# Stores moved from SyncE to ScalarE, gate loads split, and more gathers beside each u block, in a Hymba-style block with a PEER layer

## The chip, the core and the metric

The kernel runs on one core of one Trainium2 chip. The metric is the device time of one execution in microseconds (us), as the median of several runs. In what follows PE is TensorE, DVE is VectorE, ACT is ScalarE, POOL is GpSimd and SP is SyncE, which here only issues DMAs.

## What is computed

One layer on a sequence of 512 tokens with 2048 features: two mixers side by side (forgetting attention and an mLSTM), an output projection, and then a PEER layer, which is where the change lies. PEER picks, for every token, 8 × 16 = 128 of 16384 single-neuron experts, by two top-k searches over product keys:

```
q = (xt @ w_q)                                   # 8 heads, 2 halves of 128
scores = einsum('thpd,pnd->thpn', q, keys)
s_top, i_top = top_k(scores, 16)                 # per half
cand = s_top[0][:, None] + s_top[1][None, :]     # 16 x 16
s_fin, pos = top_k(cand, 16);  gate = softmax(s_fin)
ub = u[idx];  act = gelu(einsum('thkd,td->thk', ub, x)) * gate
vb = v[idx];  y = einsum('thk,thkd->td', act, vb)
out = rmsnorm(x + y)
```

`u` and `v` have 16384 rows of 2048 features.

## The kernel before, in words

The 512 tokens are NT = 4 tiles of 128. Two ways are used for PEER, side by side.

**Sparse way.** For the first tile (128 tokens) and half of the second (NS = 64 tokens) each chosen expert's row is gathered from `u`: 128 gathers for tile 0 and 64 for the half tile, which lies twice on the partitions, so 192 gathers of 128 rows of 8 KB (1 MB). The generator `gathered` (line 626) issues an indirect DMA on POOL (line 633) into one of three `row` buffers and, two steps later (LAG), a dot on DVE (line 643) that multiplies the row with the token's features and sums. Later the same generator gathers `v` rows for tile 0. `advance(n)` (line 685) moves this generator on by n steps. Each gather and each dot is tied by `beside` (line 620) to the last hi cast issued before it, so the steps go at the pace of the dense work.

**Dense way.** The remaining 320 tokens (DU) go through all experts. The experts are NI = 128 blocks of 128. A u block (`early_steps`, lines 592 to 610) streams its 2 × 512 KB of transposed `u` in two halves through `stream_split`: a raw load on SP (line 109, four `raw` buffers), a cast to the high part `hi` on ACT (line 115) and a subtraction that leaves the low part `lo` on DVE (line 117); three buffers each for hi and lo. 48 matmuls of 320 columns (line 122) add hi and lo products into a PSUM tile `sacc`. A Gelu on ACT (line 608) writes the tile `es` (two buffers), and a store puts its 160 KB into the DRAM table `stab` (line 609). Activations are needed only where a token chose an expert; this is what the gates are for.

**Gate tables.** `table` (lines 936 to 961) writes for 32 tokens (TG) a table of all 16384 gates, 2 MB, in eight groups of four tokens: an `on` on DVE (one-hot rows, line 945), four scaled copies `og` on ACT (line 950), eight small matmul records `gp` on PE, a copy into `stg` on ACT (line 953). Three u blocks are interleaved with the eight groups of a table, step by step. The table is then stored to `gtab` (line 957). There are NTG = 12 tables; the first two belong to the half tile that takes its u activations from the sparse way and can be made only when its dots are done.

**The order around the change** is this (times are of the profiled execution). The program asks for:
1. eight w_q heads with seven u blocks each, top-k searches beside them, `advance(PACE_EARLY)` per block (960 to 1506);
2. ten tables, each with three u blocks, each followed by `advance(PACE_G * 3)` (1506 to 1844);
3. u blocks alone, with `advance(PACE_U)` each, until 14 (HOLD) are left (1844 to 2018);
4. whatever is left of the u gathers, at a step per call (line 965; 2018 to 2115). The 14 held-back blocks run beside it, since the scheduler pulls them ahead;
5. the last two tables (lines 973 and 974; 2115 to 2172);
6. the transition: gates and activations come back from DRAM. `load_gates(g)` loads the gates of eight blocks (GB) of all 12 tables into `gtA` or `gtB`; `load_s(k)` loads activations of two blocks, `sv`; `gated(k)` multiplies both into `wv` (line 1000 on ACT for the two sparse tables, line 1002 on DVE for the ten) and splits it into hi and lo parts in `wbufA` or `wbufB` (lines 1006 and 1007) (2172 to 2257);
7. the v products: 16 groups of eight blocks, four `vS` raw loads per pair of blocks, split like u (2257 to 3190).

A tile scheduler fixes each engine's order at build time: it takes what is ready by its own modelled costs and priorities, so an engine's order isn't that of the code. A lo subtraction has a raised priority (AHEAD_LO). On the chip every engine runs its own list strictly in order, and waits at an instruction whose inputs or buffers aren't there. A DMA on SP's list waits in the same way, and everything behind it with it.

Of the kernel before, what the change touches and what calls it, by code (L numbers as in the profile page):

```python
# [36 lines left out]
NS = 64  # L37
# [3 lines left out]
NI = 128  # L41
GB = 8
TG = 32
# [3 lines left out]
EARLY_G = 3  # L47
HOLD = 14
PACE_O = 0.4
PACE_EARLY = 1.15  # L50
PACE_G = 1.5
PACE_U = 1.5
LAG = 2
AHEAD_LO = 35
NTG = ND // TG
# [32 lines left out]
def block_kernel(ctx: ExitStack, tc: tile.TileContext, a, out):  # L88
    nc = tc.nc
# [17 lines left out]
    def stream_split(src, width=1024, to=None):  # L107
        raw = stream.tile([P, 1024], F32, tag="raw", name="raw", bufs=4)
        nc.sync.dma_start(out=raw[:, :width], in_=src)
        if to is None:  # L110
            hi = stream.tile([P, 1024], F32R, tag="hi", name="hi", bufs=3)
            lo = stream.tile([P, 1024], F32R, tag="lo", name="lo", bufs=3)
        else:
            hi, lo = to[:, 0:1024], to[:, 1024:2048]
        pace[0] = nc.scalar.copy(out=hi[:, :width], in_=raw[:, :width]).ins  # L115
        with tc.high_priority(offset=AHEAD_LO):
            nc.vector.tensor_tensor(out=lo[:, :width], in0=raw[:, :width],  # L117
                                    in1=hi[:, :width].bitcast(F32), op=OP.subtract)
        return hi, lo

    def mm(o, l, r, start, stop):
        nc.tensor.matmul(out=o, lhsT=l, rhs=r, start=start, stop=stop)  # L122
# [441 lines left out]
    stab = gdram.tile([NI, P, DU], F32, name="stab")  # L564
    gtab = gdram.tile([NTG, P, NI * TG], F32, name="gtab")
# [4 lines left out]
    def tpool(stack, name, bufs=1, **kw):  # L570
        return stack.enter_context(tc.tile_pool(name=name, bufs=bufs, reuse_waits="tile", **kw))
# [15 lines left out]
    def flat(x):  # L587
        return x.rearrange("p h k -> p (h k)")

    nearly = [0]  # L590

    def early_steps():

        b = nearly[0]
        nearly[0] += 1
        acc = psA.tile([P, 512], F32, tag="acc", name="sacc")[:, 0:DU]
        for s in range(2):
            hi, lo = stream_split(a["uT"][b, s])
            for kk in range(8):
                kc = 8 * s + kk  # L600
                uh, ul = hi[:, kk * P:(kk + 1) * P], lo[:, kk * P:(kk + 1) * P]
                mm(acc, uh, x3d[:, 0, kc, NS:], kc == 0, False)
                mm(acc, uh, x3d[:, 1, kc, NS:], False, False)
                mm(acc, ul, x3d[:, 0, kc, NS:], False, kc == KC - 1)
                if kc % 2 == 1 and kc < KC - 1:
                    yield
        sv = esp.tile([P, DU], F32, tag="es", name="es")
        nc.scalar.activation(out=sv, in_=acc, func=AF.Gelu)
        nc.sync.dma_start(out=stab[b], in_=sv)
        yield  # L610

    def early_s():
        for _ in early_steps():
            pass
# [70 lines left out]
    def advance(n):  # L685
        state[0] += n
        while state[0] >= 1.0:
            state[0] -= 1.0
            done[0] += 1
            next(sparse, None)  # L690

    with ExitStack() as rx:
# [117 lines left out]
        def w_q(h):  # L810

            acc = [psA.tile([P, 512], F32, tag="acc", name="acc") for _ in range(2)]
            for s in range(4):
                hi, lo = stream_split(a["w_q"][h, s])
                for j in range(2):
                    for kk in range(4):
                        kc = 4 * s + kk
                        wh = hi[:, kk * 256 + j * P:kk * 256 + (j + 1) * P]
                        wl = lo[:, kk * 256 + j * P:kk * 256 + (j + 1) * P]
                        mm(acc[j][:, 0:ND], wh, x3d[:, 0, kc, :], kc == 0, False)  # L820
                        mm(acc[j][:, 0:ND], wh, x3d[:, 1, kc, :], False, False)
                        mm(acc[j][:, 0:ND], wl, x3d[:, 0, kc, :], False, kc == KC - 1)
            qT = xq.tile([P, 2, ND], F32, tag="w2", name="qT", bufs=1)
            for j in range(2):
                nc.scalar.copy(out=qT[:, j, :], in_=acc[j][:, 0:ND])
            res = {}
            for t in range(1, NT):
                sc = psB.tile([P, 2, P], F32, tag="ps", name="sc")
                for j in range(2):
                    mm(sc[:, j, :], qT[:, j, (t - 1) * P:t * P], keysT[:, j, :], True, True)  # L830
                res[t] = n2.tile([P, 2, P], F32, tag="scs", name="scs", bufs=4)
                nc.scalar.copy(out=res[t], in_=sc)
            return res
# [63 lines left out]
        for k, _ in enumerate(steps):  # L897
            next(chosen, None)
            if k % 8 == 7:
                advance(PACE_EARLY)  # L900
        for _ in chosen:
            pass
        for h in range(PH):
            scs = w_q(h)
            advance(PACE_EARLY)
            for t in range(1, NT):
                for _ in range(EARLY_TOPK[t - 1]):
                    early_s()
                    advance(PACE_EARLY)
                for _ in choose(t, h, scs[t]):  # L910
# [15 lines left out]
    with ExitStack() as rx:  # L926
        n3 = tpool(rx, "n3", 2)
        idxT = n3.tile([P, 2, ND], F32, name="idxT", bufs=1)
        gT = n3.tile([P, ND], F32, name="gT", bufs=1)
        for dst, src in ((idxT[:, 0], i0f), (idxT[:, 1], i1f), (gT, gts)):  # L930
            pt = psB.tile([P, ND], F32, tag="ps", name="pt")
            for t in range(1, NT):
                nc.tensor.transpose(pt[:, (t - 1) * P:t * P], flat(src[:, t]), ident)
            nc.scalar.copy(out=dst, in_=pt)

        def table(tg, blocks):
            stg = n3.tile([P, NI, TG], F32, tag="stg", name="stg")
            steps = itertools.chain(*[early_steps() for _ in range(blocks)])
            for q4 in range(TG // 4):
                for _ in range(blocks):  # L940
                    next(steps)
                gp_ = psB.tile([P, 4, NI], F32, tag="ps", name="gp_")
                t4 = tg * TG + q4 * 4
                on = n3.tile([P, 2, 4, P], F32, tag="on", name="on")
                nc.vector.tensor_tensor(  # L945
                    out=on, in0=iota[:, None, None, :].to_broadcast([P, 2, 4, P]),
                    in1=idxT[:, :, t4:t4 + 4, None].to_broadcast([P, 2, 4, P]), op=OP.is_equal)
                for q in range(4):
                    og = n3.tile([P, P], F32, tag="og", name="og", bufs=6)
                    nc.scalar.activation(out=og, in_=on[:, 0, q, :], func=AF.Copy,  # L950
                                         scale=gT[:, t4 + q:t4 + q + 1])
                    mm(gp_[:, q, :], on[:, 1, q, :], og, True, True)
                nc.scalar.copy(out=stg[:, :, q4 * 4:q4 * 4 + 4].rearrange("p i q -> p q i"),  # L953
                               in_=gp_)
            for _ in steps:
                pass
            nc.sync.dma_start(out=gtab[tg], in_=stg.rearrange("p i q -> p (i q)"))

        for tg in range(NS // TG, NTG):
            table(tg, EARLY_G)  # L960
            advance(PACE_G * EARLY_G)
        while nearly[0] < NI - HOLD:
            early_s()
            advance(PACE_U if not u_over[0] else 0.0)
        while not u_over[0]:
            advance(1.0)

        pt = psB.tile([P, ND], F32, tag="ps", name="pt")
        nc.tensor.transpose(pt[:, 0:P], act1, ident)
        for r in range(R):  # L970
            rs = slice(r * S1, (r + 1) * S1)
            nc.scalar.copy(out=gT[rs, 0:NS], in_=pt[rs, r * NS:(r + 1) * NS])
        for tg in range(NS // TG):
            table(tg, EARLY_G)
# [3 lines left out]
    wbufs = [va.tile([P, 2, GB, ND], F32R, name="wbufA", bufs=1), None]  # L978
    gtb = [va.tile([P, NTG, GB, TG], F32, name="gtA", bufs=1), None]

    def load_gates(g):
        gt = gtb[g % 2]
        nc.sync.dma_start(out=gt.rearrange("p g i q -> p g (i q)"),
                          in_=gtab[:, :, g * GB * TG:(g + 1) * GB * TG].rearrange("g p x -> p g x"))

    svs = {}

    def load_s(k):

        if k < NI // 2:  # L990
            svs[k] = va.tile([P, 2, DU], F32, tag="sv", name="sv", bufs=3)
            nc.sync.dma_start(out=svs[k], in_=stab[2 * k:2 * k + 2].rearrange("b p x -> p b x"))

    def gated(k):
# [11 lines left out]
        nc.scalar.copy(out=hi, in_=wv)  # L1006
        nc.vector.tensor_tensor(out=lo, in0=wv, in1=hi.bitcast(F32), op=OP.subtract)

    load_gates(0)
    while nearly[0] < NI - 2:  # L1010
        early_s()
    load_s(0)
    load_s(1)
    for k in range(2):
        gated(k)
    while nearly[0] < NI:
# [147 lines left out]
```

## Time and profile before

| what | us |
|---|---|
| median of 3 runs (3238.1 to 3244.2) | 3241.77 |
| the profiled execution | 3246.45 |
| its span | 3244.7 |
| PE busy in it | 3123.0 (96%) |
| DVE busy | 2328.5 (72%) |
| ACT busy | 1281.5 (39%) |
| POOL busy | 604.3 (19%) |

The mean granted clock of PE is 0.984 of its full rate. The stages have different limits, so the shares over the whole span say little; the times of the stages stand in the list above, and the stretches in the rows below are cut along them.

### The profile page before, as it was taken

How to read it: one execution, taken by the hardware profiler on the slowest of the kernel's cores; microseconds unless marked ns; L12 is line 12 of the kernel's file. 1: busy time of each engine (PE TensorE's matmuls, PEld its weight loads, DVE VectorE, ACT ScalarE, POOL GpSimd, SP SyncE). 2: the span in 40 equal slices, each digit the busy share in tenths (PEclk: the TensorE clock that was granted, in tenths of full speed). 3: DMA queues.
4: the chain of work that ended last, by engine and by line, in shares of the span. 5: the costliest groups of instructions: out<-in, count | busy, mean ns of one | idle time of the engine just before them, and what ended most of it. 6: DMA issues, size and time to landing. Idle time of an engine off the chain costs nothing.

```text
span 3244.7 us, 43324 instructions
## 1 busy us (share of the span) xinstructions
PE 3123.0 (96%) x16682; PEld 2752.9 (85%) x16682; DVE 2328.5 (72%) x3251; ACT 1281.5 (39%) x1957; POOL 604.3 (19%) x444
## 2 busy tenths in 40 slices
PE   8999999998989999999899899889999999999998
PEld 6788787787789999999898899877888888888887
DVE  6533333457899999898788787857778877887764
ACT  4432222345443333335777533263333333333332
POOL 0000000100322222222221233302222222222200
PEclk9999999999999999999999999989999999999999
DMA  4232232266868888887888899969988888888853
GB/s 158 72 98 78 78 97 73 78 213 201 317 238 292 298 309 294 305 285 269 320 309 328 331 408 397 387 243 340 335 310 315 324 327 319 311 317 329 300 182 118
DMA packets 220258, 835.71 MB, mean 258 GB/s; under 512 B 21586, under 2 KB 79314, under 8 KB 175954
## 3 DMA queue, kind: packets, MB, share of 16 engines
q1 hardware_dynamic: 173970, 497.38, 44.4%
q0 software_dynamic: 46080, 335.56, 26.9%
q8 instruction: 130, 2.13, 0.3%
q14 instruction: 78, 0.63, 0.1%
HBM read 781.94 MB, written 50.92 MB: 257 GB/s over the span
## 4 chain that ended last, share of the span: by engine, by line
PE 76%; issue 9%; DVE 6%; DMA 4%; POOL 2%; ACT 2%; DVEq 0%; SPq 0%; POOLq 0%; ACTq 0%
PE y L122 23%; PE acc L122 23%; PE sacc L122 17%; PE yk L122 8%; DMA row<-in_u,idx 2%; DVE lo L117 2%; POOL row L633 2%; DVE row L643 1%; PE sps L122 1%; ACT stg L953 1%; ACT og L950 1%; DMA raw<-in_w_out 1%; PE po L122 1%; ACT hi L115 1%; DMA gtA<-gtab 1%
## 5 line engine op out<-in xcount | busy, mean ns | idle before, releaser
L115 ACT CAST hi<-raw 128x1024 fp32r<-128x1024 f32 x736 | 773.6, 1051 | 1537.6 <-PE acc L122 433.3
L117 DVE TENSOR_TENSOR lo<-raw,hi 128x1024 fp32r<-128x1024 f32 x736 | 897.5, 1222 | 589.2 <-ACT hi L115 588.6
L122 PE MATMUL sacc<-x3d,hi 128*128 128x320 f32 x4096 | 934.6, 316 | 0.0
L122 PEld LDWEIGHTS sacc<-x3d,hi 128*128 128x128 f32 x4096 | 697.3, 192 | 0.0
L122 PE MATMUL sacc<-x3d,lo 128*128 128x320 f32 x2048 | 647.4, 316 | 46.1 <-DVE lo L117 45.9
L643 DVE SCALAR_TENSOR_TENSOR row<-row,x 128x2048 f32<-128x2048 f32 x192 | 437.9, 2286 | 64.9 <-DMA row<-in_u,idx 56.7
L122 PEld LDWEIGHTS sacc<-x3d,lo 128*128 128x128 f32 x2048 | 392.0, 191 | 52.1 <-DVE lo L117 52.1
L633 POOL DMA_INDIRECT row<-in_u,idx x192 | 289.9, 1510 | 670.5 <-ACT hi L115 373.5
L633 POOL DMA_INDIRECT row<-in_v,idx x128 | 224.9, 1757 | 767.7 <-ACT hi L115 540.4
L122 PE MATMUL y<-hi,wbufA 128*128 128x512 f32 x1152 | 357.4, 390 | 3.8 <-DVE x L1085 3.8
L122 PE MATMUL y<-hi,wbufB 128*128 128x512 f32 x1128 | 349.0, 389 | 0.0
L672 DVE SCALAR_TENSOR_TENSOR x<-row,dots,x 128x2048 f32<-128x2048 f32 x128 | 300.2, 2345 | 0.0
L122 PEld LDWEIGHTS y<-hi,wbufA 128*128 128x128 f32 x1152 | 217.0, 188 | 49.5 <-DVE x L1085 4.3
L122 PEld LDWEIGHTS y<-hi,wbufB 128*128 128x128 f32 x1128 | 211.7, 188 | 44.0
L122 PE MATMUL acc<-xT,hi 128*128 128x512 f32 x768 | 244.1, 396 | 0.0
L122 PE MATMUL acc<-hi,xT 128*128 128x512 f32 x768 | 241.8, 393 | 0.0
L122 PE MATMUL y<-lo,wbufA 128*128 128x512 f32 x576 | 224.8, 390 | 0.0
L122 PE MATMUL y<-lo,wbufB 128*128 128x512 f32 x564 | 219.4, 389 | 0.0
L162 POOL TENSOR_TENSOR rsr<-rst,mhalf 128x1 f32<-128x1 f32 (+2 forms) x24 | 19.0, 795 | 894.1 <-DVE rst L159 894.1
L122 PEld LDWEIGHTS acc<-xT,hi 128*128 128x128 f32 x768 | 144.2, 189 | 28.5 <-ACT xT L179 0.2
L122 PEld LDWEIGHTS acc<-hi,xT 128*128 128x128 f32 x768 | 143.8, 188 | 28.6
L945 DVE TENSOR_TENSOR on<-cst,idxT 128x1024 f32<-128x1024 f32 x96 | 117.0, 1223 | 47.6 <-PE gp__15151 L122 2.0
(545 smaller groups left out, 4168.6 us busy)
## 6 DMA issues: line engine op xcount, KB each, us to landing
raw<-in_uT SPq DMA_DIRECT2D x256, 512.0 KB
raw<-in_vS SPq DMA_DIRECT2D x256, 512.0 KB
raw<-in_w_out SPq DMA_DIRECT2D x64, 512.0 KB
raw<-in_w_q SPq DMA_DIRECT2D x64, 512.0 KB
gtab<-stg SPq DMA_DIRECT2D x12, 2048.0 KB
stab<-es SPq DMA_DIRECT2D x128, 160.0 KB
sv<-stab SPq DMA_DIRECT2D x64, 320.0 KB
raw<-in_w_fqk SPq DMA_DIRECT2D x32, 512.0 KB
```

Source lines behind the costliest of these rows:

```text
L115: pace[0] = nc.scalar.copy(out=hi[:, :width], in_=raw[:, :width]).ins
L117: nc.vector.tensor_tensor(out=lo[:, :width], in0=raw[:, :width], in1=hi[:, :width].bitcast(F32), op=OP.subtract)
L122: nc.tensor.matmul(out=o, lhsT=l, rhs=r, start=start, stop=stop)
L162: nc.gpsimd.tensor_tensor(out=r, in0=t, in1=mhalf[:, 0:width], op=OP.pow)
L633: beside(nc.gpsimd.indirect_dma_start(out=row, out_offset=None, in_=a[src], in_offset=bass.IndirectOffsetOnAxis(ap=idx(j), axis=0)))
L643: return nc.vector.scalar_tensor_tensor(out=row, in0=row, scalar=1.0, in1=x30, op0=OP.mult, op1=OP.mult, accum_out=to[:, j:j + 1])
L672: return nc.vector.scalar_tensor_tensor(out=x2[:, 0, :], in0=row, scalar=dots[0][:, j:j + 1], in1=x2[:, 0, :], op0=OP.mult, op1=OP.add)
L945: nc.vector.tensor_tensor(out=on, in0=iota[:, None, None, :].to_broadcast([P, 2, 4, P]), in1=idxT[:, :, t4:t4 + 4, None].to_broadcast([P, ...
L950: nc.scalar.activation(out=og, in_=on[:, 0, q, :], func=AF.Copy, scale=gT[:, t4 + q:t4 + q + 1])
L953: nc.scalar.copy(out=stg[:, :, q4 * 4:q4 * 4 + 4].rearrange("p i q -> p q i"), in_=gp_)
```

## The change

The stores of u blocks (line 609) and of gate tables (line 957) are issued by ACT instead of SP: 128 stores of 160 KB and 12 of 2 MB. PACE_EARLY rises from 1.15 to 1.25 gather steps per u block, PACE_G from 1.5 to 1.9. The gates of the first eight blocks are loaded in two parts: the ten tables that are made first, and, after four blocks from the end, the two last ones. The first two `sv` loads stand in the code ahead of the last blocks instead of between them.

```diff
-PACE_EARLY = 1.15
-PACE_G = 1.5
+PACE_EARLY = 1.25
+PACE_G = 1.9
@@ early_steps
         nc.scalar.activation(out=sv, in_=acc, func=AF.Gelu)
-        nc.sync.dma_start(out=stab[b], in_=sv)
+        nc.scalar.dma_start(out=stab[b], in_=sv)
@@ table
-            nc.sync.dma_start(out=gtab[tg], in_=stg.rearrange("p i q -> p (i q)"))
+            nc.scalar.dma_start(out=gtab[tg], in_=stg.rearrange("p i q -> p (i q)"))
@@ load_gates
-    def load_gates(g):
-        gt = gtb[g % 2]
+    def load_gates(g, tgs=slice(0, NTG)):
+        gt = gtb[g % 2][:, tgs]
         nc.sync.dma_start(out=gt.rearrange("p g i q -> p g (i q)"),
-                          in_=gtab[:, :, g * GB * TG:(g + 1) * GB * TG].rearrange("g p x -> p g x"))
+                          in_=gtab[tgs, :, g * GB * TG:(g + 1) * GB * TG].rearrange("g p x -> p g x"))
@@ after the tables
-    load_gates(0)
+    load_gates(0, slice(NS // TG, NTG))
+    while nearly[0] < NI - 4:
+        early_s()
+    load_gates(0, slice(0, NS // TG))
+    load_s(0)
+    load_s(1)
     while nearly[0] < NI - 2:
         early_s()
-    load_s(0)
-    load_s(1)
     for k in range(2):
         gated(k)
```

The paces and the code's order reach the engines through the scheduler. Counted in the two orders: 87 dots stand ahead of the tables before and 94 now; in the ten tables 42 (bursts of four and five in turn) and 53 (bursts of four to six, at most six); beside the dense blocks 38 in both; the leftover stretch has 25 and 7. The last two tables begin on PE at u block 123.6 before (the 16 groups within 2.4 blocks) and at 115.9 now: ten groups within 1.6 blocks, the other six some 18 u matmuls apart, and eight blocks behind the last group.

On DVE, at the end of a table with five dots before; `row` is a gathered row, `dots` the sums, `on` the one-hot rows of a gate group:

```order
L117 TENSOR_TENSOR lo<-raw,hi 128x1024
L643 SCALAR_TENSOR_TENSOR row,dots_4841<-row,x_4830 128x2048
L945 TENSOR_TENSOR on<-cst,idxT 128x1024
L117 TENSOR_TENSOR lo<-raw,hi 128x1024
L643 SCALAR_TENSOR_TENSOR row,dots_4841<-row,x_4830 128x2048
L945 TENSOR_TENSOR on<-cst,idxT 128x1024
L643 SCALAR_TENSOR_TENSOR row,dots_4841<-row,x_4830 128x2048 x3
L117 TENSOR_TENSOR lo<-raw,hi 128x1024
```

On DVE, at the end of a table with six dots now:

```order
L643 SCALAR_TENSOR_TENSOR row,dots_4841<-row,x_4830 128x2048
L945 TENSOR_TENSOR on<-cst,idxT 128x1024
L117 TENSOR_TENSOR lo<-raw,hi 128x1024
L945 TENSOR_TENSOR on<-cst,idxT 128x1024
L643 SCALAR_TENSOR_TENSOR row,dots_4841<-row,x_4830 128x2048 x3
L117 TENSOR_TENSOR lo<-raw,hi 128x1024
L643 SCALAR_TENSOR_TENSOR row,dots_4841<-row,x_4830 128x2048
L945 TENSOR_TENSOR on<-cst,idxT 128x1024
L643 SCALAR_TENSOR_TENSOR row,dots_4841<-row,x_4830 128x2048
L117 TENSOR_TENSOR lo<-raw,hi 128x1024
```

Four dots and an `on` stood between two lo's before; now three and an `on`, then a lo, then two and an `on`.

On SP, where the u blocks end, before; `raw<-in_vS` are the first loads of the v products:

```order
L957 DMA gtab<-stg 128x4096
L109 DMA raw<-in_vS 128x1024
L609 DMA stab<-es 128x320
L983 DMA gtA<-gtab 128x12x256
L992 DMA sv<-stab 128x2x320 x3
L609 DMA stab<-es 128x320
L983 DMA gtB<-gtab 128x12x256
L992 DMA sv<-stab 128x2x320 x3
L109 DMA raw<-in_vS 128x1024
```

On SP at the same place now:

```order
L983 DMA gtA<-gtab 128x12x256
L109 DMA raw<-in_vS 128x1024 x6
L983 DMA gtB<-gtab 128x12x256
L109 DMA raw<-in_vS 128x1024 x2
L992 DMA sv<-stab 128x2x320 x2
L109 DMA raw<-in_vS 128x1024
```

and, some 16 u loads ahead of that, the two parts of the first gates among the u loads:

```order
L109 DMA raw<-in_uT 128x1024 x11
L983 DMA gtA<-gtab 128x10x256
L109 DMA raw<-in_uT 128x1024
L983 DMA gtA<-gtab 128x2x256
L992 DMA sv<-stab 128x2x320 x2
L109 DMA raw<-in_uT 128x1024 x4
L992 DMA sv<-stab 128x2x320 x2
```

The `gtA` of 12 tables ahead of the six `vS` loads is that of the third group of eight blocks; the stores are gone from this list. On DVE all four `gated` pairs of the first eight blocks stand ahead of the last nine lo's of u; before they stood behind all of them.

## Rows read from the trace of the kernel before

**Rows 1.** Windows: us, PE, PEld, DVE, ACT, POOL busy (instructions), PEclk, DMA share, GB/s.
```profile
960.00:1506.00 546.00, 537.78 (x3535) 534.58 (x3536) 495.27 (x1118) 191.48 (x248) 142.69 (x147) 1.00 0.85 297
1619.00:1649.40 30.40, 29.20 (x211) 28.45 (x211) 25.59 (x23) 25.92 (x53) 8.21 (x4) 1.00 0.76 274
1649.40:1683.50 34.10, 31.24 (x210) 30.98 (x210) 27.15 (x24) 23.20 (x47) 6.25 (x5) 0.90 0.96 364
1506.00:1843.90 337.90, 308.28 (x2133) 301.77 (x2132) 262.13 (x230) 248.10 (x498) 73.92 (x44) 0.96 0.83 306
1872.50:2017.80 145.30, 144.48 (x985) 144.22 (x984) 119.76 (x105) 51.13 (x65) 55.14 (x32) 1.00 1.01 402
2017.80:2115.10 97.30, 80.37 (x484) 77.79 (x483) 78.55 (x70) 24.33 (x31) 33.23 (x22) 0.91 0.97 381
2115.10:2172.00 56.90, 53.32 (x362) 48.87 (x360) 30.12 (x27) 46.14 (x99) 1.80 (x1) 1.00 0.56 202
2172.00:2257.10 85.10, 70.83 (x289) 57.44 (x290) 59.83 (x54) 28.25 (x41) 16.11 (x9) 0.90 0.97 349
```
**Rows 2.** Windows of the tile sacc alone: PE, PEld, ACT, PEclk, DMA share, GB/s.
```profile
1506.00:1843.90 337.90, 258.07 (x1493) 229.12 (x1492) 13.77 (x32) 0.96 0.83 306
2017.80:2115.10 97.30, 80.37 (x484) 77.79 (x483) 4.30 (x10) 0.91 0.97 381
2115.10:2172.00 56.90, 44.01 (x233) 35.06 (x231) 2.13 (x5) 1.00 0.56 202
```
**Rows 3.** Chain of work that ended last: start, us, engine, tile, line, instructions.
```profile
1044.47 48.54 PE sacc L122 x331
...
2273.43 48.96 PE y L122 x216
```
**Rows 4.** Timeline of PE, a gate group: start, us, engine, line, operation.
```profile
1517.82 1.05 PE L122 MATMUL gp__13556<-og,on 128*128 128x128 f32 x8
1518.63 0.54 PE L122 MATMUL sacc<-x3d,hi 128*128 128x320 f32 x2
```
**Rows 5.** Timeline of DVE in a table with four dots.
```profile
1630.63 1.22 DVE L117 TENSOR_TENSOR lo<-raw,hi 128x1024 fp32r<-128x1024 f32 x1
...
1639.61 1.22 DVE L117 TENSOR_TENSOR lo<-raw,hi 128x1024 fp32r<-128x1024 f32 x1
```
**Rows 6.** Timeline of DVE in the next table, with five dots; idle before in brackets.
```profile
1659.23 1.22 DVE L117 TENSOR_TENSOR lo<-raw,hi 128x1024 fp32r<-128x1024 f32 x1
...
1667.50 2.29 DVE L643 SCALAR_TENSOR_TENSOR row<-row,x 128x2048 f32<-128x2048 f32 x1 [1.49 <-DMA row<-in_u,idx]
...
1671.00 2.29 DVE L643 SCALAR_TENSOR_TENSOR row<-row,x 128x2048 f32<-128x2048 f32 x1 [1.20 <-DMA row<-in_u,idx]
...
1673.21 1.22 DVE L117 TENSOR_TENSOR lo<-raw,hi 128x1024 fp32r<-128x1024 f32 x1
```
**Rows 7.** Timeline of PE behind that.
```profile
1674.49 0.64 PE L122 MATMUL sacc<-x3d,lo 128*128 128x320 f32 x1 [2.86 <-DVE lo L117]
```
**Rows 8.** Timeline of POOL in the same table: a gather's issue.
```profile
1662.93 1.67 POOL L633 DMA_INDIRECT row<-in_u,idx  x1 [2.81 <-DVE row L643]
```
**Rows 9.** SP: its waits for Gelu (total, times, longest); timeline in that table.
```profile
SPq L609 <- ACT es L608: 170.5, 72, 7.3
...
1649.88 0.33 SPq L609 DMA_DIRECT2D stab<-es  x1
1650.30 6.03 SPq L109 DMA_DIRECT2D raw<-in_uT  x3
...
1669.11 0.33 SPq L957 DMA_DIRECT2D gtab<-stg  x1
```
**Rows 10.** Timelines at the transition, of PE, ACT and SP.
```profile
2181.57 0.80 PE L122 MATMUL yk<-hi,wbufA 128*128 128x512 f32 x1 [10.39 <-ACT wbufA L1006]
...
2177.63 0.50 ACT L1000 COPY wv<-gtA 128x128 f32<-128x128 f32 x2 [5.17 <-DMA gtA<-gtab]
...
2173.99 0.43 SPq L983 DMA_DIRECT2D gtB<-gtab  x1
2185.83 0.46 SPq L109 DMA_DIRECT2D raw<-in_vS  x1
```

## The prediction, made before the changed kernel was run

> **What bounds the kernel now.** I read the page's busy shares first, then the table of time windows by stage, then the chain of waits and the timelines around the waits. TensorE is busy nearly all the time, so the question for each stage is how much longer it lasts than its matmuls need. The units come from long unbroken runs in the chain [rows 3]: 48.54 us for 331 u matmuls is 146.6 ns each, so a u block of 48 takes 7.04 us; 48.96 us for 216 v products is 226.7 ns each. A gate group between u matmuls takes 1518.63 − 1517.82 = 0.81 us [rows 4], a table of eight 6.5 us. By these units [rows 1, 2]:
> - ten tables: 337.9 − 1493 × 0.1466 (218.9) − 10 × 6.5 = 54 us over;
> - dense u blocks: 145.3 for 985 matmuls, 1 us over. Here TensorE is the bound and the gathers beside it (1.5 per block) are free;
> - leftover gathers, 2.5 per block: 97.3 − 484 × 0.1466 (71.0) = 26.3 us over, with the DMA share at 0.97: bound by bytes;
> - last two tables: 56.9 − 233 × 0.1466 (34.2) − 13 = 9.7 us over;
> - transition to the v products: 85.1 − 289 × 0.2267 (65.5) = 19.6 us over.
> The two table rows of 30.4 and 34.1 us [rows 1] are a table with four dots and one with five. One more dot costs 3.7 us there. The timelines say how. In the four-dot table VectorE's longest way between two lo's is 1630.63 to 1639.61, three dots and an `on` [rows 5]; in the five-dot one it is 1659.23 to 1673.21, four dots, of which the last two wait 1.49 and 1.20 us for their rows [rows 6]. TensorE uses up its lo's and pauses 2.86 us [rows 7], and the granted clock of that table is 0.90 instead of 1.00 [rows 1]: if it fell from 2.4 to 1.2 GHz behind the pause, it stayed there for a fifth of 34.1 us and lost half of these 6.8. The pause and 3.4 make 6.3, and the table is over by as much: of its 210 matmuls 64 are of gate groups, and 34.1 − 146 × 0.1466 − 6.5 = 6.2. So the price is that of a pause, not of a dot.
>
> **The change part by part.** Sums are made against the profiled execution, 3246.45 us, which is 4.7 above the median of 3241.77; the forecast starts from the median.
>
> *The stores on ScalarE.* They leave SP's queue, where they waited 170.5 us for Gelu [rows 9] with the raw loads behind them. In the stages that cost nothing visible: three raw loads pass right behind a store [rows 9], and where TensorE stops it waits for lo, not for raw. So the gain in the stages is 0. On ScalarE each store stands right behind the Gelu or the copy that makes its data, so the wait is the engine's own order and only the issue is added, 0.33 us by SP's row [rows 9]. What is queued behind it is the next hi cast, for which lo and then TensorE wait. In the tables about 40 stores make 13 us of work on an engine that is busy 248.1 of 337.9 [rows 1]. From below 0, since it idles 90 us there; from above 13, if each lies in the way. I take a third of the 13, **+4**, as the stops go back to VectorE. Elsewhere ScalarE has over half its time free: 0.
>
> *More gathers beside the w_q heads.* The order has 94 dots ahead of the tables instead of 87: seven more of 2.29 us [rows 6] on a VectorE that is busy 495.27 of 546 [rows 1]. TensorE idles 8.2 us there with 51 us free on VectorE; 16 fewer free add about a quarter, **+2** (0, covered, to 8, doubled).
>
> *More gathers in the ten tables:* 53 dots instead of 42, in bursts of 4 to 6. At 3.7 us each the 11 cost 41, the upper bound. The lower is −8: the order puts a lo after three dots, so the long way of 14 us that made the pauses is gone, and a six-dot table may run like the four-dot one. Between them I take the wait for a row that a late dot shows, 1.20 us [rows 6], VectorE's 2.29 beside it being hidden as in the four-dot table: 11 × 1.2 = **+13**.
>
> *Dense blocks:* 38 dots in both orders, **0**.
>
> *Leftover:* 7 dots instead of 25. The stage loses 26.3/25 = 1.05 us per dot, 18 fewer give **−19** (−24, if so few no longer fill the queues; −14, if the rest run slower). The blocks that run there now run beside the last tables or as dense ones, at 7.04 us: no cost.
>
> *Last two tables:* they begin on TensorE at block 115.9 instead of 123.6; 10 of the 16 groups are still crowded into 1.6 blocks, 6 stand apart among u matmuls. I leave 10/16 of the 9.7: **−4** (−10 to 0).
>
> *First gates in two parts, sv loads earlier.* TensorE's stop of 10.39 us comes from the first wbufA [rows 10], for which ScalarE waited 5.17 us on gtA. In the new order VectorE makes all four pairs of the first eight blocks ahead of the last nine lo's; their weights are ready some four blocks early, and the 10.39 go. The other 9.2 stand beside SP's queue: after a store and gtB at 2173.99, the next vS load comes at 2185.83 [rows 10], though lo's free its buffers sooner. In the new order six vS loads stand ahead of gtB. Most of that goes: **−16** (−8, if the second part waits for its table; −20, all). When it is gone the v products' own TensorE rate is next. The second part waits on SP for the last table's store, with the sv loads and four raw loads queued behind it; the last group is some two blocks (14 us) ahead of it, so I cost that at nothing, and it is a rival.
>
> *Sum:* 2 + 13 + 4 + 0 − 19 − 4 − 16 = **−20**; 3241.8 − 20 = **3222 us**.
>
> **The rivals.**
> (a) *The finer interleave makes the added dots free:* no pause as long as 2.86 us, the clock stays. Tables and stores cost 0: 3222 − 17 = **3205**. For: the granted clock is 1.00 in the four-dot table, whose run of dots is as long as the new one. Against: six rows of 1 MB come within about one block and three row buffers.
> (b) *Every added dot brings its 3.7 us:* 41 in place of 13, 3222 + 28 = **3250**, slower. The place is the end of each table. It decides from 33 us for the 11 dots, 3.0 each, where nothing is left of the gain; from 39.5 it measures as slower. For: the measured step from four to five. Against: it counts one pause, which the new order breaks.
> (c) *The stores, on a queue of their own, stretch the gathers.* A row asked for at 1662.93 [rows 8] is used at 1671.00 [rows 6], 8.07 us later, while raw loads and gathers fill the DMA to 0.96 [rows 1]. A gather that shares with two others and not with one takes half as long again, 12.1: 4.0 us at each of ten tables, 3222 + 40 = **3262**. It decides from (20 + 6.5)/10 = 2.7 us a table. Against: the 2 MB store of a table goes out at 1669.11 [rows 9], when all but the last of the burst's rows are asked for. The Trainium skill, page "DMA: Bandwidth & Descriptors", section "Queues, rings and completion order", states that a DMA engine takes turns between the queue rows that have work, packet by packet, and that ScalarE's row is another than SP's. By that rule the store no longer stands in line with the raw loads but takes a share from the gathers; no row here shows ScalarE's row at work. The same page, section "Issuing engines are not separate DMA queues", expects of such a move only the issue time, and speaks against (c) as much as against any gain from the stores.
> (d) *The end doesn't gain:* SP stands at the second part of the gates until the last store has landed, raw loads and vS loads come late behind it; the transition gives 8, the tables 0: 3222 + 12 = **3234**.
> That the change would not do what it says is no case here: the order shows every move.
>
> **How the numbers follow.** The forecast has 0.44, (a) 0.20, (b) 0.18, (c) 0.08, (d) 0.10. A measurement of this kernel tells about 0.2%, 6.5 us, from no change, so faster is below 3235.3 and slower above 3248.3. Faster: 0.41 of the forecast, 0.20, 0.01 of (b), 0.05 of (d), 0.67. Same: 0.03, 0.08 of (b) and 0.05 of (d), 0.16. Slower: 0.09 of (b) and (c), 0.17. The range runs from 3195, (a) with the tail's terms at their best ends, to 3255, (b) with its spread; it leaves out (c), some of (b) and a little below.
>
> **What would show it.** In the changed kernel's windows: the stretch at 2.5 gathers per block shrinks to some 28 us; the stop ahead of the first v product is under 2 us and no vS load is late behind gtB; tables with six dots take 32 to 36 us. A clock of 0.90 in every table and stops on lo of 3 us speak for (b); the same tables at 30 to 31 us for (a); waits of 3 us and more of dots for their rows, with the store of the table under way, for (c); SP standing at the second gates for (d). Wrong altogether would be a loss in a stage that I cost at nothing: the dense blocks, or the v products, which the change leaves alone.

## The result and the profile after

The changed kernel takes 3285.2 us (3284.3 to 3289.0, 4 runs) against 3240.8 before (3238.1 to 3244.2, 4 runs): a ratio of 1.0139, 95% interval 1.0121 to 1.0156. It is 44 us slower; 20 us faster was forecast. The profiled execution has a span of 3287.2 us.

First, where the time went. The ten tables can be cut in both kernels from their first to their last gate group. These are windows of the kernel before, then of the one after; the columns are those of [rows 1].

```profile
1512.30:1832.70 320.40, 293.95 (x2047) 287.97 (x2047) 254.86 (x223) 241.44 (x487) 73.06 (x43) 0.96 0.83 306
```
```profile
960.00:1506.00 546.00, 540.77 (x3538) 536.71 (x3537) 508.36 (x1128) 190.99 (x248) 175.00 (x153) 0.99 0.86 310
1512.70:1902.70 390.00, 314.77 (x2023) 301.92 (x2023) 274.80 (x241) 238.60 (x487) 88.59 (x52) 0.89 0.76 278
1928.00:2103.00 175.00, 170.35 (x1152) 168.58 (x1151) 140.17 (x124) 58.09 (x72) 63.34 (x38) 1.00 1.00 390
2103.00:2125.00 22.00, 17.56 (x101) 17.02 (x99) 17.54 (x17) 6.16 (x12) 3.42 (x3) 0.84 0.90 320
2125.00:2172.00 47.00, 44.30 (x316) 42.19 (x316) 26.52 (x22) 42.59 (x90) 0.00 (x0) 1.00 0.49 176
2172.00:2229.00 57.00, 57.00 (x391) 56.98 (x390) 25.96 (x24) 23.99 (x34) 1.80 (x1) 1.00 0.86 299
2229.00:2314.00 85.00, 81.72 (x357) 66.43 (x356) 64.43 (x56) 29.28 (x39) 18.52 (x11) 1.00 0.94 344
```

The tables take 390.0 us instead of 320.4, with a granted clock of 0.89 instead of 0.96. Of the 70 us, 49 are time in which TensorE stands still (75 us now, 26 before), and 21 are longer busy time at the lower clock. Everything else is within a few us of before, or better. The w_q stage ends at the same time. The 24 u blocks behind the tables take 175 us (172 before). The stretch of the leftover gathers is 22 us long instead of 97. The last two tables lose under 3 us, and the eight blocks behind them run without a stop; and in the 85 us from the first v product on, 357 matmuls go through where 289 did in the 85.1 us of [rows 1]. From u block 90 to the first v product it is 2228.8 − 1928 = 301 us, before 2181.6 − 1852 = 330. So 29 us are won there, and 5 in the v products (1049 us to the last one, 1054 before). What stands on the other side is 70 us in the tables, and 6 more up to block 90.

Next, what TensorE waits for in the tables. These are the waits of the window above, after (total, times, longest); before, these three were 42.4, 18.7 and 18.5 us.

```profile
ACT og L950 <- DVE on L945: 69.0, 16, 11.2
DVE row L643 <- DMA row<-in_u,idx: 60.6, 22, 5.6
...
PE sacc L122 <- DVE lo L117: 47.6, 13, 7.0
```

The dots wait for their rows. One table shows the chain. First VectorE, then TensorE, then POOL and ScalarE, all after:

```profile
1658.58 2.29 DVE L643 SCALAR_TENSOR_TENSOR row<-row,x 128x2048 f32<-128x2048 f32 x1 [1.61 <-DMA row<-in_u,idx]
...
1660.80 1.22 DVE L117 TENSOR_TENSOR lo<-raw,hi 128x1024 fp32r<-128x1024 f32 x1
1665.10 2.29 DVE L643 SCALAR_TENSOR_TENSOR row<-row,x 128x2048 f32<-128x2048 f32 x1 [3.09 <-DMA row<-in_u,idx]
...
1667.32 1.22 DVE L945 TENSOR_TENSOR on<-cst,idxT 128x1024 f32<-128x1024 f32 x1
1673.99 2.29 DVE L643 SCALAR_TENSOR_TENSOR row<-row,x 128x2048 f32<-128x2048 f32 x1 [5.45 <-DMA row<-in_u,idx]
...
1676.21 1.22 DVE L117 TENSOR_TENSOR lo<-raw,hi 128x1024 fp32r<-128x1024 f32 x1
```
```profile
1669.03 1.47 PE L122 MATMUL gp__14850<-og,on 128*128 128x128 f32 x8 [3.18 <-ACT og L950]
1677.49 0.64 PE L122 MATMUL sacc<-x3d,lo 128*128 128x320 f32 x1 [6.99 <-DVE lo L117]
```
```profile
1658.08 0.94 POOL L633 DMA_INDIRECT row<-in_u,idx  x1 [0.30 <-issue]
...
1659.38 0.33 ACTq L957 DMA_DIRECT2D gtab<-stg  x1
```

Between the lo at 1660.80 and the one at 1676.21 VectorE has only two dots and an `on`, 5.8 us of work, and takes 15.4, longer than the four dots of [rows 6]. The row asked for at 1658.08 is used at 1673.99, 15.9 us later; in [rows 6, 8] it was 8.07. The table's 2 MB store went out 1.3 us behind the gather. TensorE pauses 6.99 us and then runs at half rate: in the trace the next u matmuls are 0.27 us apart and not 0.147, and the granted clock from 1677.4 to 1680.4 is 0.50, the lower level, 1.2 GHz.

### The profile page after: what moved, and what is told of

It reads as the page before. It is cut to its first block, busy times and chain, and to the rows that moved or that the text cites. A ratio compares the mean times of both kernels' runs of the same rounds, so it can differ in the third digit from the quotient of the medians.

```text
span 3287.2 us, 43229 instructions
## 1 busy us (share of the span) xinstructions
PE 3134.8 (95%) x16682; PEld 2763.0 (84%) x16682; DVE 2326.3 (71%) x3251; ACT 1278.5 (39%) x1957; POOL 626.2 (19%) x444
## 3 DMA queue, kind: packets, MB, share of 16 engines
q10 hardware_dynamic: 20160, 46.15, 3.6%
## 4 chain that ended last, share of the span: by engine, by line
PE 73%; issue 10%; DMA 7%; DVE 6%; POOL 2%; ACT 1%; DVEq 0%; POOLq 0%; SPq 0%; ACTq 0%
PE acc L122 23%; PE y L122 23%; PE sacc L122 15%; PE yk L122 7%; DMA row<-in_u,idx 5%; DVE lo L117 2%; POOL row L633 1%; DVE row L643 1%; DMA raw<-in_uT 1%; PE sps L122 1%; PE po L122 1%; DMA raw<-in_vS 0%; DMA gtB<-gtab 0%; PE sc L122 0%; PE gps L122 0%
## 5 line engine op out<-in xcount | busy, mean ns | idle before, releaser
L633 POOL DMA_INDIRECT row<-in_u,idx x192 | 298.4, 1554 | 675.1 <-ACT hi L115 340.3
```

The costliest lines, as they stand in the source:

```text
L633: beside(nc.gpsimd.indirect_dma_start(out=row, out_offset=None, in_=a[src], in_offset=bass.IndirectOffsetOnAxis(ap=idx(j), axis=0)))
```

## The experiments

Two causes were put against each other. **Q**: a table's store and the gathers share the DMA in the same 15 us, and a dot that is wanted at once waits for its row. **D**: each added dot costs its own time. A third came up on the way. **T**: with DMAs on ScalarE's list the scheduler makes another order there, and the hi casts come late. The table is from one profile and 4 to 10 timed runs of each kernel; the ratios are to runs of the kernel before in the same series, with medians of 3242.2 to 3244.1 us (the changed kernel's is to the 3240.8); "tables" is the time from the first to the last gate group of the ten; dots are the dots in that stretch.

| kernel | stores issued by | table store goes out | dots | tables, us | median, us | ratio to before (95%) |
|---|---|---|---|---|---|---|
| before | SP | table's end | 42 | 320 | 3240.8 | 1 |
| changed | ACT | end | 52 | 390 | 3285.2 | 1.0139 (1.0121 to 1.0156) |
| e1_stores | ACT | end | 42 | 362 | 3297.4 | 1.0171 (1.0154 to 1.0188) |
| g2_gtab | ACT for tables, SP for u | end | 42 | 342 | 3284.8 | 1.0130 (1.0107 to 1.0153) |
| e3_gates | SP | end | 42 | 318 | 3245.6 | 1.0003 (0.9993 to 1.0014) |
| e4_gtab_sp | SP for tables, ACT for u | end | 52 | 368 | 3259.8 | 1.0048 (1.0032 to 1.0065) |
| e7_sp_all | SP | end | 52 | 375 | 3261.3 | 1.0059 (1.0040 to 1.0078) |
| e8_sp_pg15 | SP | end | 41 | 327 | 3238.0 | 0.9986 (0.9975 to 0.9996) |
| f1_stores_mid | ACT | third group of the next table | 42 | 392 | 3329.6 | 1.0258 (1.0231 to 1.0286) |
| f2_all_mid | ACT | third group | 51 | 393 | 3291.5 | 1.0141 (1.0124 to 1.0158) |
| f3_sp_mid | SP | third group | 52 | 342 | 3226.7 | 0.9941 (0.9924 to 0.9957) |
| f4_before_mid | SP | third group | 42 | 332 | 3257.9 | 1.0054 (1.0037 to 1.0071) |
| f5_sp_mid4 | SP | fifth group | 52 | 351 | 3241.0 | 0.9994 (0.9982 to 1.0006) |
| p1_nosplit_mid | SP | third group | 52 | 339 | 3228.2 | 0.9957 (0.9939 to 0.9974) |
| h1_stores_hi | ACT, hi casts raised | end | 42 | 334 | 3264.4 | 1.0069 (1.0050 to 1.0088) |
| h2_stores_mid_hi | ACT, hi casts raised | third group | 42 | 358 | 3289.0 | 1.0148 (1.0131 to 1.0166) |
| h3_all_mid_hi | ACT, hi casts raised | third group | 52 | 370 | 3263.8 | 1.0075 (1.0056 to 1.0093) |
| h4_changed_hi | ACT, hi casts raised | end | 53 | 371 | 3264.1 | 1.0064 (1.0042 to 1.0086) |

**One part at a time.** The stores alone, against the kernel before:

```diff
-        nc.sync.dma_start(out=stab[b], in_=sv)
+        nc.scalar.dma_start(out=stab[b], in_=sv)
-            nc.sync.dma_start(out=gtab[tg], in_=stg...)
+            nc.scalar.dma_start(out=gtab[tg], in_=stg...)
```


> The kernel before with the two kinds of stores on ScalarE and nothing else; the ten tables keep their 42 dots. Theory Q (the table's 2 MB store, on a queue of its own, shares the DMA with the gathers and stretches them): the rows asked for beside a table's store land after 12 to 16 us as in the changed kernel, the ten tables grow by 30 to 50 us, about 3280 us in all. Theory D (each added dot costs some 4 to 6 us of TensorE, whoever issues the stores): no added dots, so the tables stay at about 338 us and the total at 3241, within 6.

They cost 55 us, with not one dot more. So a good part isn't D. A row of VectorE in this kernel shows Q at work:

```profile
1682.03 1.22 DVE L117 TENSOR_TENSOR lo<-raw,hi 128x1024 fp32r<-128x1024 f32 x1
1691.03 2.29 DVE L643 SCALAR_TENSOR_TENSOR row<-row,x 128x2048 f32<-128x2048 f32 x1 [7.78 <-DMA row<-in_u,idx]
```

This row was asked for at 1675.49, 2.6 us ahead of the table's store. In the kernel before, too, a gather was asked for 2.8 us ahead of a store, but its dot came 25 us later: with the stores on ScalarE the scheduler made another order on VectorE as well, though with as many dots. And the dots of this kernel wait 43 us in all, 24 more than before, while its tables are 42 us longer: Q need not be the whole.

The gate and sv loads alone (the last part of the diff, the rest as before):

> The kernel before with the split gate loads and the earlier sv loads alone. Both theories: nothing moves in the ten tables; the stop of 10.4 us ahead of the first v product is shorter, 3227 to 3236 us. If the stop stays, 3241: then the earlier start of the last tables, and not the split, is what gave the changed kernel its faster end.

Nothing. Both theories expected a gain at the transition. In this kernel TensorE stands still for 9.1 us between the last u matmul and the first v product, 10.4 before.

The changed kernel with the table stores back on SP, and with both kinds back on SP:

```diff
-            nc.scalar.dma_start(out=gtab[tg], in_=stg...)
+            nc.sync.dma_start(out=gtab[tg], in_=stg...)
```


> The changed kernel with the table stores back on SyncE; the 160 KB stores stay on ScalarE, and the ten tables have the changed kernel's dots. Theory Q: the tables lose most of their 70 us of growth, the total is 3220 to 3240. Theory D: the dots are the same, so about 3285. A third, S (any store on ScalarE's queue does the harm, the small ones too): 3260 to 3285.

```diff
-        nc.scalar.dma_start(out=stab[b], in_=sv)
-            nc.scalar.dma_start(out=gtab[tg], in_=stg...)
+        nc.sync.dma_start(out=stab[b], in_=sv)
+            nc.sync.dma_start(out=gtab[tg], in_=stg...)
```


> The changed kernel with both kinds of stores back on SyncE: only the paces and the gate loads are changed against the kernel before. Theory Q and S: the stretch of the gathers is gone, 3215 to 3235, by the sum of the prediction without its term for the stores. Theory D: 53 dots still stand in the ten tables, about 3285.

Both lie between the theories, at 3260 and 3261: 24 to 25 us come back, and 17 to 19 stay. With the new paces and every store on SP the tables still take 375 us. So the paces cost by themselves, and the small stores on ScalarE cost nothing beside them. The table stores alone on ScalarE, against the kernel before:

```diff
-            nc.sync.dma_start(out=gtab[tg], in_=stg...)
+            nc.scalar.dma_start(out=gtab[tg], in_=stg...)
```


> The kernel before with the table stores alone on ScalarE; the 160 KB stores stay on SyncE. Theory Q: all of the 55 us of the two stores together, 3285 to 3300, since only the 2 MB store is long enough to stretch a gather. If the small stores had a part, less: 3245 to 3280.

3284.8, at the edge of what Q expects; the small stores add 13 us to it when they move too. But the dots wait only 28 us for rows here, 9 more than before, and the tables take 22 of the 41 us: Q isn't the whole here either.

**The place of the store.** If it is the overlap in time, another place for the store must help, whoever issues it. Here the store is held back until the third gate group of the next table is copied, when the burst is over (and, in f3 and f4, 2 to 5 us before the next one begins); first the stores alone on ScalarE, then the changed kernel, then the same with SP:

```diff
+        waiting = []
+        def store_table(after=None):
+            if waiting:
+                wt, ws = waiting.pop()
+                st = nc.scalar.dma_start(out=gtab[wt], in_=ws...)      # nc.sync in f3, f4, f5
+                if after is not None:
+                    tc.add_manual_dep(st.ins, after.ins.name, ...)
...
-                nc.scalar.copy(out=stg[...], in_=gp_)
+                cp = nc.scalar.copy(out=stg[...], in_=gp_)
+                if q4 == 2:                                            # 4 in f5
+                    store_table(cp)
...
-            nc.sync.dma_start(out=gtab[tg], in_=stg...)
+            waiting.append((tg, stg))
```


> The stores alone on ScalarE (3297 us), but a table's 2 MB store is held back until the third gate group of the next table is copied, when the gathers of the burst are through. Theory Q (the store and the gathers share the DMA in the same 15 us, whichever queue issues them, and a dot that is wanted at once waits): the gathers wanted at once land in 8 to 10 us, the tables go from 362 back to 320 to 330, 3243 to 3260 us. Theory R (ScalarE's queue itself, or the issue on ScalarE, costs the time): the tables stay at 350 to 365, 3285 to 3300.

> The changed kernel (3285 us) with the table stores held back in the same way. Theory Q: the tables go from 390 to 340 to 355, 3235 to 3255 us. Theory R: 3275 to 3290. If added dots cost 3.7 us each by themselves, the tables keep 41 us of growth, about 3250 to 3260.

> The new paces and gate loads with both stores on SyncE (3261 us), the table stores held back in the same way. Theory Q: the queue doesn't matter, the tables go from 375 to 340 to 355, 3225 to 3245 us. Theory R says nothing of it; by theory D (each added dot costs its own time) nothing moves, 3255 to 3265.

With SP it does what Q says: 3261.3 to 3226.7, tables 375 to 342, and this kernel is 0.6% faster than the one before. The DMA views of the ten tables, e7 and then f3 (issues, size, median from issue to landing), show it: the store and the rows land sooner, and the dots' waits fall from 52.6 to 30.6 us.

```profile
gtab<-stg SPq DMA_DIRECT2D x10, 2048.0 KB, 13.4
...
row<-in_u,idx POOLq DMA_INDIRECT x54, 10.0
```
```profile
gtab<-stg SPq DMA_DIRECT2D x9, 2048.0 KB, 7.4
...
row<-in_u,idx POOLq DMA_INDIRECT x53, 9.0
```

This is the cleanest of the comparisons. Through the first seven tables VectorE, ScalarE and TensorE have the same order in e7 and f3; only SP's differs, by the store's place and the loads around it. These seven tables take 261 us in e7 and 238 in f3. Of their gathers, e7 asks for 14 within 4 us of a store: they land after 13.8 us in the median, and their dots wait 22.3 us. The same gathers in f3 land after 9.0, and their dots wait 1.1. One of these dots, in e7 and then in f3:

```profile
1667.14 2.29 DVE L643 SCALAR_TENSOR_TENSOR row<-row,x 128x2048 f32<-128x2048 f32 x1 [4.89 <-DMA row<-in_u,idx]
```
```profile
1650.63 2.29 DVE L643 SCALAR_TENSOR_TENSOR row<-row,x 128x2048 f32<-128x2048 f32 x1
```

With ScalarE it does nothing (f2) or harm (f1, 32 us more). In f1 the store lands after 6.7 us in the tables and the dots wait 30 us instead of 43, yet the tables take 392. That is against Q. ScalarE's timeline in f1 points to another cause:

```profile
1661.65 1.05 ACT L115 CAST hi<-raw 128x1024 fp32r<-128x1024 f32 x1 [2.37 <-PE sacc L122]
1666.51 1.28 ACT L962 ACTIVATE og<-on,gT 128x128 f32<-128x128 f32 x4 [3.81 <-DVE on L957]
1669.74 1.11 ACT L965 COPY stg<-gp__14813 128x512 f32<-128x512 f32 x1 [1.95 <-PE gp__14813 L122]
...
1681.59 1.05 ACT L965 COPY stg<-gp__14932 128x512 f32<-128x512 f32 x1 [3.51 <-PE gp__14932 L122]
1682.44 0.67 ACT L962 ACTIVATE og<-on,gT 128x128 f32<-128x128 f32 x2
1683.02 0.41 ACT L608 ACTIVATE es<-sacc 128x320 f32<-128x320 f32 x1
1683.34 1.03 ACT L115 CAST hi<-raw 128x1024 fp32r<-128x1024 f32 x1
```

Between two hi casts lie 21.7 us. Four gate groups, two of which wait for TensorE or VectorE by some us, stand ahead of the second in ScalarE's list. In f1's tables TensorE waits 8.8 us for hi, which it never does before, and 37.5 for lo instead of 18.5. The longest such stretch that ends in a table is 6 to 15 us before, 9 to 21 with the stores alone on ScalarE, 20 to 25 in nine of f1's ten tables, and 10 to 21 in the changed kernel. The list is made by the scheduler; the stores changed it. The length of the stretch alone doesn't set the time: in g2 it is 7 to 21 us, and the tables take 342.

The kernel before with its stores on SP held back, and the new paces with the store held back two groups longer:

> The kernel before with the table stores on SyncE held back to the middle of the next table, nothing else; VectorE's order of dots is the same. Theory Q: in the kernel before no row that is wanted at once was asked for beside a store, so nothing is gained, 3238 to 3246. If holding back the store is a gain by itself, 3210 to 3230, and the new paces then cost nothing in the tables.

> New paces and gate loads, stores on SyncE, a table's store held back until the fifth group of the next table and not the third (3227 us). Theory Q: farther from the burst behind and not yet at the one ahead, the same or a little better, 3218 to 3232. If the overlap moves to the next burst: 3240 to 3260.

f4 is 16 us slower, which no theory had. VectorE's, ScalarE's and TensorE's orders in the tables are exactly those of the kernel before, so only the store's place differs, with SP's loads around it, and the result fits Q: the store now goes out 2 to 4 us ahead of the next burst's first gather, and the dots wait 27.9 us for rows instead of 18.7. In the kernel before, the gathers asked for within 4 us of a store were used 20 to 28 us later. f5 gives back what f3 won, as was expected for an overlap with the next burst: its store goes out among that burst's first gathers, and its dots wait 38.0 us, not 30.6. So the place of the store decides by tens of us, and the good place depends on where the bursts are.

**ScalarE's order.** To test T the hi casts of the ten tables get a raised priority, so that the scheduler spreads them; the stores stay on ScalarE, at the end or held back.

```diff
+HI_UP = [0]
...
-        pace[0] = nc.scalar.copy(out=hi[:, :width], in_=raw[:, :width]).ins
+        with tc.high_priority(offset=HI_UP[0]):
+            pace[0] = nc.scalar.copy(out=hi[:, :width], in_=raw[:, :width]).ins
...
+        HI_UP[0] = 60
         for tg in range(NS // TG, NTG):
             table(tg, EARLY_G)
             advance(PACE_G * EARLY_G)
+        HI_UP[0] = 0
```


> The stores alone on ScalarE (3297 us), with a raised priority for the hi casts of the ten tables, so that ScalarE's order spreads the casts over a table instead of bunching them in its last third; the store stays at the table's end. Theory T (the stores on ScalarE's list changed the order that the scheduler makes there, hi casts come late and lo and TensorE with them): tables from 362 to 325 to 340, total 3250 to 3270. Theory Q (only the DMA overlap of store and gathers costs): 3285 to 3300.

> The stores alone on ScalarE with the table store held back to the middle of the next table (3330 us), with the raised priority of the hi casts. Theory T: the overlap is gone already and the order now too, tables from 392 to 320 to 335, total 3240 to 3260. Theory Q alone can't explain the 3330 and expects no change.

> The changed kernel with the table stores held back (3291 us) and the raised priority of the hi casts. Theory T: tables from 393 to 340 to 355, as with the stores on SyncE held back, total 3225 to 3245. If ScalarE's queue costs by itself, 3260 or more stays.

> The changed kernel with the raised priority of the hi casts alone; stores on ScalarE, the table store at the table's end. Theory T (ScalarE's order): the share that ScalarE's list has in the changed kernel goes, tables from 390 to 365 to 378, 3255 to 3272. If the order has no part there: 3280 to 3290.

All four are faster for it: 33 us with the stores alone, 41 with them held back, 28 and 21 in the changed kernel with and without the hold. The tables lose 28, 34, 23 and 19 us. In h2 the longest stretch between hi casts is 14 us. Windows of the tables, of e1 and then of h1, with the same dots and the store at the same place:

```profile
1509.70:1872.00 362.30, 308.44 (x2048) 298.86 (x2048) 254.90 (x223) 237.72 (x487) 68.46 (x43) 0.92 0.72 268
```
```profile
1509.80:1843.60 333.80, 300.99 (x2048) 289.75 (x2048) 254.93 (x223) 236.11 (x487) 75.69 (x43) 0.95 0.82 293
```

In h1 TensorE waits 10.1 us for lo, in e1 32.5. So the order that the scheduler makes is a cause, and the raised priority takes back 28 of e1's 42 us in the tables. That it is ScalarE's list by itself isn't shown. Each gather and dot is tied to a hi cast, so VectorE's order changed along with it, and h1's dots wait 27 us for rows where e1's wait 43. And no run raises the hi casts with the stores on SP, so what the priority gives to any kernel isn't known. The order isn't all of it either: h2 and h3 were expected at 3225 to 3260 and stay 31 and 37 us above f4 and f3, their like on SP. Whether that rest is the issues on ScalarE's list (40 of 0.33 us, 13 us), other differences of order, or the queue itself, the runs don't tell apart.

**The dots, and the split.**

```diff
-PACE_G = 1.9
+PACE_G = 1.5
```


> Both stores on SyncE, split gate loads, PACE_EARLY 1.25, but PACE_G 1.5 as before. If the added dots in the tables cost the 55 us there (kernel with 1.9: 3261 us), the tables fall from 375 to 320 to 335 and the end keeps most of its gain: 3215 to 3235. If the order of the tables is spoilt by something else, they stay above 350: 3250.

```diff
-    load_gates(0, slice(NS // TG, NTG))
-    while nearly[0] < NI - 4:
-        early_s()
-    load_gates(0, slice(0, NS // TG))
-    load_s(0)
-    load_s(1)
+    load_gates(0)
     while nearly[0] < NI - 2:
         early_s()
+    load_s(0)
+    load_s(1)
```


> New paces, stores on SyncE held back to the third group, but the gate and sv loads as before. If the split brings the end's gain, 3240 to 3250 (the 10 us stop ahead of the v products and the late vS loads are back). If the earlier last tables bring it, 3225 to 3232 as with the split.

e8: without the added dots in the tables these take 327 us, and 48 of the 55 us are back: 4.4 us for each of the 11 dots. The total is 3238, a little above what was expected, since with more dots left over the way from block 90 to the first v product is 311 us and not e7's 296. p1: without the split loads the held-back kernel is as fast as with them, 3228 and 3227. So the end's gain belongs to the paces, and not to the split.

## Why the prediction was wrong

**The end was right in size.** −19 for the leftover gathers, −4 for the last tables and −16 for the transition, 39 in all, were forecast; 29 up to the first v product and 5 in the v products came. The leftover stretch is over its matmuls by 7 us (22.0 − 101 × 0.1466) instead of 26, as forecast. The stop of 10.39 us [rows 10] is gone:

```profile
2228.64 0.31 PE L122 MATMUL sacc<-x3d,lo 128*128 128x320 f32 x1
2228.79 0.39 PE L122 MATMUL yk<-hi,wbufA 128*128 128x512 f32 x1
```

But the reason given for the 16 was wrong, and its size was luck. The split loads bring nothing (e3, p1). It is the gathers that end sooner: the last two tables then are done eight blocks before the end, and the gates are in DRAM in time, loaded in one part or in two.

**w_q and dense** were right: 0 for a forecast +2, and 3 us for 0.

**The ten tables were wrong: +17 forecast, +70 measured.** Three steps failed.

- *The dots, +13.* With all stores on SP they cost 55 us (e7 against before; 48 against e8, which differs in PACE_G alone). The step took the wait of a late row, 1.20 us, as the price of an added dot, and argued that a lo after three dots ends the long way of 14 us. The order did become finer, and the way in the table shown became longer all the same: 15.4 us with two dots, since the landing of its rows set its length, and not the number of its dots. Holding the table's store back takes 33 of the 55 away (375 to 342), 23 of them in the seven tables whose order on the compute engines is the same; so the larger part is the store beside rows that are wanted at once, an overlap that the step put at nothing. The rest, some 2 us a dot, is near the 1.2 taken; what it is made of wasn't tested. The lower bound of −8 was worked out from no row. Rival (b) came nearest in size (3.7 each; 4.4 to 5 measured), but not the mechanism: nothing in it spoke of the store.
- *The stores, +4 with 0 from below and 13 from above.* In the changed kernel they add 24 us over e7, 15 of them in the tables, and alone 55, 42 of them in the tables. The bounds were those of a DMA issue, 0.33 us on a list that stays as it was. The list didn't stay: the step counted what the stores put into ScalarE's order and not what the scheduler moved around them, there and on VectorE. ScalarE's order was there to be read, and the prediction read VectorE's and SP's. How much of the 15 us in the changed kernel is the order and how much the rows, which wait 8 us more than in e7, isn't separated.
- *Rival (c)* named the store and the rows, at 4.0 us a table, 3262, and put its cause in a queue of its own. The overlap is real, and the queue isn't its cause: with the store on SP it lands after 13.4 us (e7) and on ScalarE after 14.5 (changed kernel), and in e7 rows wait as well. The trace does show a row of its own for ScalarE (q10, 46.15 MB, the size of its 140 stores, absent before), as the Trainium skill, page "DMA: Bandwidth & Descriptors", section "Queues, rings and completion order", states; that a DMA engine takes turns between the rows by packets would fit the small difference, but no run shows it. The argument against (c), that the store goes out when the burst is nearly through, held for the order before and not for the new one, where two dots of the burst stand behind the store.

The same page of the Trainium skill, section "Issuing engines are not separate DMA queues", expects of DMAs on several engines only a saving of issue time. The measurement is otherwise: the move of 140 issues, 46 us at 0.33 us each over the whole kernel, cost 55 us, and the tables alone, with 40 of them (13 us), lost 42.

**Rival (d)** did not come: SP's second part of the gates goes out 0.05 us behind the raw load ahead of it and holds nothing up.

```profile
2183.77 0.62 SPq L109 DMA_DIRECT2D raw<-in_uT  x1
2184.44 0.42 SPq L983 DMA_DIRECT2D gtA<-gtab  x1
2184.96 1.38 SPq L992 DMA_DIRECT2D sv<-stab  x2
```

**What stays open:** what the raised priority gives by itself, and with it ScalarE's share in the order's cost; the 31 to 37 us between h2 and f4, and h3 and f3; and why the small stores on ScalarE cost 13 us in one order (e1 against g2) and none in another (e4 against e7). The version that beats both kernels is the paces with the table's store held back on SP, 3227 to 3228 us, with or without the split.

## What to carry to other kernels

Where a scheduler sets the order, moving a DMA to a busy engine is first a change of order, on that engine and on those tied to it: read the new lists around it for the operations that feed the bound engine, and price their delay, not the issue. A large store beside gathers cost time here where a consumer wanted a row at once, so put it where the rows that land with it aren't wanted for a while, and check the place again whenever the pace of the gathers changes. An argument that counts instructions between two marks holds only as long as none of them waits.

## What the runs showed of the hardware

In the ten tables a store of 2 MB to DRAM landed after some 7 us away from the gathers' burst (7.4 in f3, 6.7 in f1) and after 12 to 15 beside a burst of 1 MB gathers (12.7 in e3, 13.4 in e7, both issued by SP; 14.5 in the changed kernel). A gather asked for within 4 us of it took 13 to 15 us in the median (13.0 in e3, 13.8 in e7, 14.0 in the changed kernel, 14.8 in e4), the others 8 to 9. In the kernel with only the gate loads changed, whose order in the tables is that of the kernel before, 8 of 43 gathers took over 12 us too, and their dots didn't wait: in the tables these came 22 to 28 us after the request. Behind the pause of 6.99 us TensorE's matmuls came at the lower of its two rates for about 3 us (granted clock 0.50); in the kernel before, behind the 2.86 us of [rows 7], for about 6 (0.50 from 1674.4 to 1680.6).
